# Projections with PSUM banks taken singly, the rotary embedding in two operations, and one operation less in the roots

## The chip, the cores and the metric

One core of a Trainium2 chip runs the whole kernel. The metric is the device time of one execution in microseconds. TensorE (PE) multiplies out of SBUF into PSUM, which has eight banks of 512 float32 columns; VectorE (DVE) and ScalarE (ACT) read PSUM; GpSimd (POOL) works in SBUF only here; SyncE (SP) issues nearly all of the transfers.

## The reference

Two encoder layers on 1024 tokens of width 1024. Each layer normalises its input and projects it with one matrix of 2848 columns, whose columns belong to three kinds of attention: latent attention (6 heads, with a second projection from a rank of 384 for the queries and 256 for keys and values), differential attention (4 heads with two maps each) and grouped-query attention with a rotary embedding in two axes (6 query heads, 2 key heads). Queries and keys are normalised per head and rotated:

```python
def _rms_norm(x, gain):
    y = xf * lax.rsqrt(jnp.mean(xf * xf, axis=-1, keepdims=True) + EPS)
    return (y * gain).astype(x.dtype)

def _apply_rope(x, cos, sin):
    half = x.shape[-1] // 2
    x1, x2 = xf[..., :half], xf[..., half:]
    return jnp.concatenate([x1 * cos - x2 * sin, x1 * sin + x2 * cos], axis=-1)

for l in range(DEPTH):
    h = _rms_norm(x, attn_norm[l]) @ w_in[l]
    (h_cq, h_ckv, h_kr, h_dq, h_dk, h_dv, h_gq, h_gk, h_gv) = jnp.split(h, IN_OFFSETS, axis=-1)
    ...
    x = x + mix @ w_o[l]
    gate, up = jnp.split(_rms_norm(x, ffn_norm[l]) @ w_gate_up[l], 2, axis=-1)
    x = x + (jax.nn.silu(gate) * up) @ w_down[l]
```

The attentions are dense softmax attentions without a mask, with scale width^-0.5.

## The kernel before, in words

Each float32 operand of a large product is split into a high part of TensorE's rounded float32 type and the rest, and `mm3` (line 162) issues three matmuls: rest by high, high by rest, high by high. They have the lines 164, 165 and 166 in the profile.

A layer has four stages in this order: the projections, the attention, the output projection, and the feed-forward part (whose products are arranged so that seven block products do the work of eight). The change lies in the projections, and in small operations elsewhere.

**Projections.** The tokens lie in 8 tiles of 128. `x_features` (244) transposes the input in 8 pieces for each half of the tokens: four 128 by 128 transposes into one PSUM bank (`pt`, line 248), then ACT writes the high part (250) and DVE the rest (251, tile `xl`). `weights` (225) loads two k-tiles of a weight slice at a time on SP's queue (232), ACT casts the high part (`wh`, through `split`, line 123) and POOL or DVE makes the rest (`wl`, line 124). `project` (302) then takes the token tiles in pairs: for both it issues all matmuls over k into the two halves of one PSUM tile of two banks (`psb`), and then calls `emit` for both. `emit` is the reader of the projection. In `heads64` (404) it is: ACT copies PSUM to `raw` with the row's scale (415), DVE rotates (349 and 351), POOL adds the two rotary products (418), ACT squares (419), DVE sums the squares per head (420), and, for the grouped-query slice that also carries values, ACT and DVE write the values' two parts from PSUM (437, 438). In `mla_q` (490) it is ACT's copy (499), POOL's gain (504), the rotary, POOL's sum (512), and the squares. `mla_kv` (523) reads keys by 537 and values by 123 and 124 (tile `vst`). `down` (453) reads by DVE (461), and the shared rotary key goes through `kr_extra` (553).

After each half of the tokens `finish` (383) takes the root of the mean squares and POOL multiplies it on (391). `out_features`, which transposes the result for the attention (368) and stores it in two parts (ACT 372, DVE 373, tiles `sth` and `stl`, transfers 381), is put off: `project` calls it once LAG steps of later products have been issued. `neg_lambda` (178) makes one small product per layer.

**The rotary** (`rope`, 344): `dst = raw * C` in one DVE operation, and `tmp` = the swapped halves by the signed sine in two operations, one for each half. `rotate64` (396) calls it for each group of 2 × `half` columns of a head of 64, so once for a differential head (half 32) and twice for a grouped-query head (half 16).

**The roots** (`newton`, 126): a first guess by integer operations (132, 133), h = -0.5 v (135), and three steps of r·r, times h, and (t + 1.5)·r (138, 139, 140), all dependent, on DVE. With `eng` given (the outputs of the differential heads) the steps run on POOL with four operations a step and no h. `rsq` (148) makes v = ssq / n + eps (151) and calls it; `finish` multiplies the attention's scale on in an operation of its own (389).

**PSUM.** One pool at a time holds the eight banks. `psum(2, 2)` for the projections: two tiles `s` of two banks for the products, two banks `t` for the transposes of `out_features`, two banks `o`; `x_features` takes `o` and `t` in turn, `neg_lambda` takes `o`. `psum(3, 1)` (637) for the attention. `psum_one()` (989) for the rest: three banks `u` and five banks `v`; its tiles are used singly. At the layer's end `psum(2, 2)` comes again (1325).

**What sets the order.** Each engine works through its instructions in a fixed order, laid out when the program is built: the framework places instructions by the program's order and by when their inputs and buffers come free on a simulated timeline. SP's transfers are in a fixed order too. Work buffers of the projections are two deep (`raw`, `tmp`, `vst`), the weights' parts six.

Of the kernel before, what the change touches and what calls it, by code (L numbers as in the profile page):

```python
# [12 lines left out]
F32 = mybir.dt.float32  # L13
# [3 lines left out]
ALU = mybir.AluOpType  # L17
# [3 lines left out]
P = 128  # L21
# [44 lines left out]
def encoder(ctx: ExitStack, tc: tile.TileContext, a: dict, out: bass.AP):  # L66
# [22 lines left out]
    def ps_o(name, n=512):  # L89
        return banks["pool"].tile([P, n], F32, tag="o", name=name, bufs=banks["o"])  # L90

    def psum_one():

        banks["pool"].release()
        banks["pool"] = tc.alloc_tile_pool(name="psu", bufs=3, space=PSUM, reuse_waits="tile")

    def ps_u(name):
# [28 lines left out]
    def newton(pool, v, n, tag, eng=None):  # L126

        i = pool.tile([P, n], I32, tag=tag + "i", name="i")
        h = pool.tile([P, n], F32, tag=tag + "h", name="h")
        t = pool.tile([P, n], F32, tag=tag + "t", name="t")  # L130
        r = pool.tile([P, n], F32, tag=tag + "r", name="r")
        ve.tensor_scalar(i, v.bitcast(I32), 1, None, ALU.arith_shift_right)
        ve.tensor_scalar(r.bitcast(I32), i, -1, 0x5F3759DF, ALU.mult, ALU.add)
        if eng is None:
            ve.tensor_scalar(h, v, -0.5, None, ALU.mult)
        for _ in range(3):
            if eng is None:
                ve.tensor_tensor(out=t, in0=r, in1=r, op=ALU.mult)
                ve.tensor_tensor(out=t, in0=t, in1=h, op=ALU.mult)
                ve.scalar_tensor_tensor(out=r, in0=t, scalar=1.5, in1=r, op0=ALU.add, op1=ALU.mult)  # L140
            else:
                eng.tensor_tensor(out=t, in0=r, in1=r, op=ALU.mult)
                eng.tensor_tensor(out=t, in0=t, in1=v, op=ALU.mult)
                eng.tensor_scalar(t, t, -0.5, 1.5, ALU.mult, ALU.add)
                eng.tensor_tensor(out=r, in0=t, in1=r, op=ALU.mult)
        return r

    def rsq(pool, ssq, n, inv, scale, tag):

        v = pool.tile([P, n], F32, tag=tag + "v", name="v")  # L150
        ve.tensor_scalar(v, ssq, inv, EPS, ALU.mult, ALU.add)
        r = newton(pool, v, n, tag)
        if scale != 1.0:
            ve.tensor_scalar(r, r, float(scale), None, ALU.mult)
        return r

    def gain_cols(src, n, name):
        t = lay.tile([P, n], F32, tag=name, name=name)
# [19 lines left out]
    def neg_lambda(l):  # L178
        lam_init = 0.8 - 0.6 * math.exp(-0.3 * l)
        lq = lay.tile([64, 4], F32, tag="lq", name="lq")  # L180
        for i, n in enumerate(("diff_lq1", "diff_lq2", "diff_lk1", "diff_lk2")):
            sy.dma_start(out=lq[:, i : i + 1], in_=a[n][l].unsqueeze(1))
        lp = lay.tile([64, 2], F32, tag="lp", name="lp")
        ve.tensor_mul(lp, lq[:, 0:2], lq[:, 2:4])
        pl_ = ps_o("pl_")
        pe.matmul(pl_[:, 0:2], ones[:64, :], lp, start=True, stop=True)
        le = lay.tile([P, 2], F32, tag="le", name="le")
        ac.activation(le, pl_[:, 0:2], AF.Exp)
        nlam = lay.tile([P, 1], F32, tag="nlam", name="nlam")
        ve.tensor_tensor(out=nlam, in0=le[:, 1:2], in1=le[:, 0:1], op=ALU.subtract)  # L190
        ve.tensor_scalar(nlam, nlam, -lam_init, None, ALU.add)
        return nlam

    psum(2, 2)
    def rows_by_quarters(t):

        return lambda tt, c0, c1: t[tt // 4][c0 // 512][:, tt % 4, c0 % 512 : (c1 - 1) % 512 + 1]
# [5 lines left out]
    for l in range(L):  # L203
# [39 lines left out]

        def x_features(g):
            for j in range(KT):
                pt = ps_t("pt") if j % 2 else ps_o("pt")
                for i in range(4):
                    pe.transpose(pt[:, i * P : (i + 1) * P], Xv(4 * g + i, j * P, (j + 1) * P), ident)
                h, lo = (t[:, j, :] for t in XT[g])
                ac.activation(h, pt, AF.Copy, scale=g_attn[:, j : j + 1])  # L250
                ve.scalar_tensor_tensor(
                    out=lo, in0=pt, scalar=g_attn[:, j : j + 1], in1=f(h), op0=ALU.mult, op1=ALU.subtract
                )
# [48 lines left out]
        def project(x, nk, w, n, emit):  # L302
            (xh, xl), (wh, wl) = x, w
            for tp in range(TT // 2):
                ps = ps_s("psb")
                for i in range(2):
                    for k in range(nk):
                        mm3(
                            ps[:, i, :n], xh(k, 2 * tp + i), xl(k, 2 * tp + i), wh[k], wl[k],
                            k == 0, k == nk - 1,  # L310
                        )
                for i in range(2):
                    emit(2 * tp + i, ps[:, i, :n])
                for e in list(later):
                    e[0] -= nk * n
                    if e[0] < 0:
                        later.remove(e)
                        e[1]()
                yield
# [24 lines left out]
        def rope(raw, half, C, Sn, dst, tmp):  # L344

            shape = list(raw.shape)
            C, Sn = (t.unsqueeze(1).to_broadcast(shape) for t in (C, Sn))
            cut = slice(0, half), slice(half, 2 * half)
            ve.tensor_tensor(out=dst, in0=raw, in1=C, op=ALU.mult)
            for c in range(2):  # L350
                ve.tensor_tensor(
                    out=tmp[:, :, cut[c]], in0=raw[:, :, cut[1 - c]], in1=Sn[:, :, cut[c]], op=ALU.mult
                )

        def work(name, n, most=384):
            return bp.tile([P, n], F32, tag=name, name=name, padded_shape=[P, most])
# [6 lines left out]

        def out_features(g, t, pieces, gains=None):
            for j, (c0, w, rows) in enumerate(pieces):
                pt = ps_t("pt")
                for i in range(4):
                    pe.transpose(pt[:w, i * P : (i + 1) * P], t[:, i, c0 : c0 + w], ident)
                h = bp.tile([P, 512], F32R, tag="sth", name="sth")[:w]
# [13 lines left out]
        def finish(g, t, ssq, nh, width, pieces, scaled):  # L383

            n = 4 * nh
            r = rsq(bp, ssq.rearrange("p t h -> p (t h)"), n, 1.0 / width, 1.0, "q")
            if scaled:
                rv = r.rearrange("p (t h) -> p t h", h=nh)[:, :, :scaled]
                ve.tensor_scalar(rv, rv, float(width**-0.5), None, ALU.mult)
            tv = t.rearrange("p t (h x) -> p (t h) x", x=width)  # L390
            po.tensor_tensor(
                out=tv, in0=tv, in1=r.unsqueeze(2).to_broadcast([P, n, width]), op=ALU.mult
            )
            later.append([LAG, lambda: out_features(g, t, pieces)])

        def rotate64(raw, t, tmp, h0, h1, C, Sn, half, tt):
            for b in range(0, 64, 2 * half):
                rv, tv, mv = (
                    x.rearrange("p (h x) -> p h x", x=64)[:, h0:h1, b : b + 2 * half]
                    for x in (raw, t, tmp)  # L400
                )
                rope(rv, half, C[:, tt, b : b + 2 * half], Sn[:, tt, b : b + 2 * half], tv, mv)

        def heads64(col, nh, extra, tables, half, pieces, scaled, emit_extra=None):

# [916 lines left out]
                        sy.dma_start(out=out[0, r0 : r0 + P, cs], in_=x)  # L1322
        op_.release()
        fp.release()
        psum(2, 2)
        if l < L - 1:
            xin = dram.tile([S, D], F32, tag="xs", name="xs", bufs=1)
            for r in range(2):
# [29 lines left out]
```

## Time and profile before

| | us |
|---|---|
| median of three runs | 3275.53 |
| lowest and highest | 3267.33, 3277.81 |
| the profiled execution | 3267.01 |
| its span, first to last instruction | 3265.2 |

The profile shows one execution. The busy line gives each engine's busy time, its share of the span and its instructions. A row of busy time by stretches gives the same for a part of the span, and the clock that TensorE was granted there as a share of full speed. In the waits and in brackets in the timeline stands how long an engine was idle before an instruction, and what ended that. In the timeline a row with x2 is two instructions of one kind in a row. The first layer's projections run from the start to about 400 us, the second layer's from about 1640 to 2022 us.

### The profile page before, as it was taken

Reading aid. Unit: us, or ns where it says so; the run is one execution under the profiler, and the core shown is the slowest. Engines: PE = TensorE matmul, PEld = TensorE weight load, DVE = VectorE, ACT = ScalarE, POOL = GpSimd, SP = SyncE. Lnnn points to the kernel's source line nnn. Section 1 sums busy time; section 2 is a strip of 40 time slices with the busy share of each in tenths; the row PEclk is TensorE's granted clock in tenths of the full one; section 3 lists DMA queues with packets and bytes.
Section 4 is the critical chain, followed back from the end, with each engine's and each line's share of the span. In section 5 each row is a group of like instructions: output and inputs, shape, how many; then the busy total and the mean of one; then the engine's idle time right before and its main releaser. Section 6 shows DMA issues by size and latency. Waiting matters only on the chain.

```text
span 3265.2 us, 50229 instructions
## 1 busy us (share of the span) xinstructions
PE 3096.9 (95%) x17628; PEld 2712.1 (83%) x17628; DVE 2319.8 (71%) x4560; ACT 1586.5 (49%) x3010; POOL 1139.7 (35%) x1562
## 2 busy tenths in 40 slices
PE   8889899999998999989998888999999989999999
PEld 7888888888787888878887888888887878888787
DVE  5976788888537656667669777888884476656776
ACT  4433378887424333333343344888773343333332
POOL 1633477777302001000026344777772021001000
PEclk9999999999999999999999999999999999999999
DMA  4565534333662333374344656434346523334632
GB/s 145 162 202 172 177 118 129 113 105 113 217 220 76 102 97 101 116 263 143 97 136 150 191 179 189 122 112 118 109 142 207 187 74 105 109 97 160 221 134 100
DMA packets 386076, 466.17 MB, mean 143 GB/s; under 512 B 36768, under 2 KB 275360, under 8 KB 385824
## 3 DMA queue, kind: packets, MB, share of 16 engines
q1 hardware_dynamic: 372416, 418.38, 41.3%
q0 software_dynamic: 13408, 44.57, 4.1%
q8 instruction: 140, 2.29, 0.3%
q14 instruction: 112, 0.92, 0.1%
HBM read 313.42 MB, written 149.42 MB: 142 GB/s over the span
## 4 chain that ended last, share of the span: by engine, by line
PE 76%; DVE 11%; DMA 5%; ACT 3%; issue 3%; POOL 1%; SPq 1%; ACTq 0%; DVEq 0%; POOLq 0%
PE sc L688 8%; PE pv L897 8%; PE ptc L711 5%; PE psa L164 5%; PE psa L166 5%; PE psa L165 5%; PE psb L164 4%; PE psb L165 4%; PE psb L166 4%; PE psy L166 4%; PE psy L165 4%; PE psy L164 4%; PE psc L166 2%; PE psc L164 2%; PE psc L165 2%
## 5 line engine op out<-in xcount | busy, mean ns | idle before, releaser
L688 PE MATMUL sc<-k,q 128*128 128x512 f32 (+1 forms) x1472 | 418.6, 413 | 14.7 <-ACT p L696 14.1
L695 DVE TENSOR_REDUCE nm<-sc 128x1 f32<-128x1024 f32 x320 | 389.7, 1218 | 56.9 <-PE sc L688 53.8
L164 PE MATMUL psb<-wh,xl 128*128 128x256 f32 (+2 forms) x1280 | 388.9, 305 | 40.2 <-DVE vst L438 12.8
L696 ACT ACTIVATE p<-sc,nm 128x1024 f32<-128x1024 f32 x320 | 359.0, 1122 | 61.6 <-DVE nm L695 48.7
L165 PE MATMUL psb<-wl,xh 128*128 128x256 f32 (+2 forms) x1280 | 386.2, 302 | 2.5 <-POOL wl L124 2.0
L166 PE MATMUL psb<-wh,xh 128*128 128x256 f32 (+2 forms) x1280 | 384.6, 300 | 0.0
L717 DVE TENSOR_TENSOR pl<-ptc,ph 128x512 fp32r<-128x512 f32 x512 | 336.7, 681 | 28.0 <-ACT ph L716 26.3
L716 ACT CAST ph<-ptc 128x512 fp32r<-128x512 f32 x512 | 287.4, 587 | 79.1 <-PE ptc L711 70.8
L688 PEld LDWEIGHTS sc<-k,q 128*128 128x128 f32 (+1 forms) x1472 | 257.9, 191 | 63.5 <-ACT p L696 24.2
L711 PE MATMUL ptc<-ident,p 128*128 128x128 f32 x2048 | 290.9, 275 | 12.0 <-DVE pl L717 6.5
L897 PE MATMUL pv<-ph,v 128*128 128x256 f32 x1280 | 299.4, 286 | 0.0
L164 PEld LDWEIGHTS psb<-wh,xl 128*128 128x128 f32 x1280 | 249.8, 196 | 44.5 <-issue 13.4
L897 PE MATMUL pv<-pl,v 128*128 128x256 f32 x1024 | 275.4, 294 | 8.4 <-DVE ot L763 6.4
L711 PEld LDWEIGHTS ptc<-ident,p 128*128 128x128 f32 x2048 | 241.0, 142 | 46.2 <-DVE pl L717 6.3
L1229 POOL DMA_DIRECT2D hd<-h x66 | 36.1, 547 | 680.0 <-DVE h L1170 434.3
L164 PE MATMUL psy<-bh,al 128*128 128x512 f32 x616 | 240.9, 394 | 14.9 <-DVE al L124 14.9
L165 PEld LDWEIGHTS psb<-wl,xh 128*128 128x128 f32 x1280 | 249.7, 195 | 3.8 <-POOL wl L124 2.8
L751 POOL TENSOR_SCALAR p<-p,rec 128x1024 f32<-128x1024 f32 x192 | 215.7, 1127 | 104.5 <-DVE rec L701 83.4
L166 PEld LDWEIGHTS psb<-wh,xh 128*128 128x128 f32 x1280 | 249.4, 195 | 0.0
L165 PE MATMUL psy<-bl,ah 128*128 128x512 f32 x616 | 241.2, 392 | 0.1
L166 PE MATMUL psy<-bh,ah 128*128 128x512 f32 x616 | 240.4, 391 | 0.0
L123 ACT CAST wh<-ws 128x512 fp32r<-128x512 f32 x176 | 108.6, 623 | 265.1 <-PE psa L166 236.4
(223 smaller groups left out, 7687.5 us busy)
## 6 DMA issues: line engine op xcount, KB each, us to landing
graw<-in_w_gate_up SPq DMA_DIRECT2D x88, 512.0 KB, 5.4
ar<-hd SPq DMA_DIRECT2D x28, 1024.0 KB, 6.1
hd<-hs POOLq DMA_DIRECT2D x88, 256.0 KB, 3.1
hd<-h POOLq DMA_DIRECT2D x66, 256.0 KB, 2.4
q<-qd SPq DMA_DIRECT2D x256, 64.0 KB, 2.4
B<-od SPq DMA_DIRECT2D x12, 1280.0 KB, 7.0
wraw<-in_w_in SPq DMA_DIRECT2D x56, 256.0 KB, 3.2
o<-od SPq DMA_DIRECT2D x10, 1280.0 KB, 11.0
```

Of the source, the lines that this page charges most:

```text
L123: (hi_eng or ac.copy)(h, src)
L164: pe.matmul(ps, xl, wh, start=first, stop=False, skip_group_check=more)
L165: pe.matmul(ps, xh, wl, start=False, stop=False, skip_group_check=more)
L166: pe.matmul(ps, xh, wh, start=False, stop=last, skip_group_check=more)
L688: pe.matmul(ps[:, half, :], q[x][:, cut], kk[y], start=at == 0, stop=at == len(products) - 1)
L695: ve.tensor_reduce(nm, pf, axis=AX.X, op=ALU.max, negate=True)
L696: ac.activation(p, pf, AF.Exp, bias=nm, accum_out=s)
L711: pe.transpose(pt[:, k * P : (k + 1) * P], p[:, (4 * b + k) * P : (4 * b + k + 1) * P], ident)
L716: ac.copy(h, pv)
L717: ve.tensor_tensor(out=pl[:, 4 * b : 4 * b + 4, i * P : (i + 1) * P], in0=pv, in1=f(h), op=ALU.subtract,)
L751: po.tensor_scalar(p, p, r, 1.0, ALU.mult, ALU.mult)
L897: pe.matmul(b.o, x, y, start=first, stop=last)
```

## The change

Four edits:

- PSUM: `project` takes one bank `v` for each token tile (five deep) in place of a half of a tile of two banks (two deep). All transposes of the projections and the product of `neg_lambda` take banks `u` (three deep). The pool `psum_one` now serves the projections, too, and stays from the output projection of one layer to the projections of the next.
- Rotary: the two operations for the halves become one, which reads the halves in reversed order; `rotate64` calls `rope` once for 64 columns, so that the product with C is one operation for the whole head, and for a half of 16 two reversed ones follow.
- Roots on DVE: -0.5 goes into the first operation of a step, and h is gone.
- Scale: `rsq` folds a scale into v, so that `finish` needs operation 389 only where it applies to some of the heads.

```diff
     def psum_one():
-        banks["pool"].release()
+        if banks:
+            banks["pool"].release()
...
     def newton(pool, v, n, tag, eng=None):
-        h = pool.tile([P, n], F32, tag=tag + "h", name="h")
...
-        if eng is None:
-            ve.tensor_scalar(h, v, -0.5, None, ALU.mult)
         for _ in range(3):
             if eng is None:
-                ve.tensor_tensor(out=t, in0=r, in1=r, op=ALU.mult)
-                ve.tensor_tensor(out=t, in0=t, in1=h, op=ALU.mult)
+                ve.scalar_tensor_tensor(out=t, in0=r, scalar=-0.5, in1=r, op0=ALU.mult, op1=ALU.mult)
+                ve.tensor_tensor(out=t, in0=t, in1=v, op=ALU.mult)
                 ve.scalar_tensor_tensor(out=r, in0=t, scalar=1.5, in1=r, op0=ALU.add, op1=ALU.mult)
...
     def rsq(pool, ssq, n, inv, scale, tag):
-        ve.tensor_scalar(v, ssq, inv, EPS, ALU.mult, ALU.add)
-        r = newton(pool, v, n, tag)
-        if scale != 1.0:
-            ve.tensor_scalar(r, r, float(scale), None, ALU.mult)
-        return r
+        ve.tensor_scalar(v, ssq, inv / scale**2, EPS / scale**2, ALU.mult, ALU.add)
+        return newton(pool, v, n, tag)
...
-        pl_ = ps_o("pl_")
+        pl_ = ps_u("pl_")
...
-    psum(2, 2)
+    psum_one()
...
-                pt = ps_t("pt") if j % 2 else ps_o("pt")
+                pt = ps_u("pt")
...
-                ps = ps_s("psb")
+                ps = [ps_v("psb")[:, :n] for _ in range(2)]
                 for i in range(2):
                     for k in range(nk):
                         mm3(
-                            ps[:, i, :n], xh(k, 2 * tp + i), xl(k, 2 * tp + i), wh[k], wl[k],
+                            ps[i], xh(k, 2 * tp + i), xl(k, 2 * tp + i), wh[k], wl[k],
                             k == 0, k == nk - 1,
                         )
                 for i in range(2):
-                    emit(2 * tp + i, ps[:, i, :n])
+                    emit(2 * tp + i, ps[i])
...
         def rope(raw, half, C, Sn, dst, tmp):
             shape = list(raw.shape)
-            C, Sn = (t.unsqueeze(1).to_broadcast(shape) for t in (C, Sn))
-            cut = slice(0, half), slice(half, 2 * half)
-            ve.tensor_tensor(out=dst, in0=raw, in1=C, op=ALU.mult)
-            for c in range(2):
-                ve.tensor_tensor(
-                    out=tmp[:, :, cut[c]], in0=raw[:, :, cut[1 - c]], in1=Sn[:, :, cut[c]], op=ALU.mult
-                )
+            n = shape[2]
+            ve.tensor_tensor(out=dst, in0=raw, in1=C.unsqueeze(1).to_broadcast(shape), op=ALU.mult)
+            for b in range(0, n, 2 * half):
+                cut = (slice(None), slice(None), slice(b, b + 2 * half))
+                rv, tv = (t[cut].rearrange("p h (c x) -> p h c x", c=2) for t in (raw, tmp))
+                sv = Sn[:, b : b + 2 * half].rearrange("p (c x) -> p c x", c=2).unsqueeze(1)
+                ve.tensor_tensor(out=tv, in0=rv[:, :, ::-1, :], in1=sv.to_broadcast(list(rv.shape)), op=ALU.mult)
...
         def out_features(g, t, pieces, gains=None):
-                pt = ps_t("pt")
+                pt = ps_u("pt")
...
         def finish(g, t, ssq, nh, width, pieces, scaled):
-            r = rsq(bp, ssq.rearrange("p t h -> p (t h)"), n, 1.0 / width, 1.0, "q")
-            if scaled:
+            whole = width**-0.5 if scaled == nh else 1.0
+            r = rsq(bp, ssq.rearrange("p t h -> p (t h)"), n, 1.0 / width, whole, "q")
+            if 0 < scaled < nh:
...
         def rotate64(raw, t, tmp, h0, h1, C, Sn, half, tt):
-            for b in range(0, 64, 2 * half):
-                rv, tv, mv = (
-                    x.rearrange("p (h x) -> p h x", x=64)[:, h0:h1, b : b + 2 * half]
-                    for x in (raw, t, tmp)
-                )
-                rope(rv, half, C[:, tt, b : b + 2 * half], Sn[:, tt, b : b + 2 * half], tv, mv)
+            rv, tv, mv = (x.rearrange("p (h x) -> p h x", x=64)[:, h0:h1, :] for x in (raw, t, tmp))
+            rope(rv, half, C[:, tt, :], Sn[:, tt, :], tv, mv)
...
         op_.release()
         fp.release()
-        psum(2, 2)
         if l < L - 1:
```

## The prediction

> **What bounds the kernel now.** I read the page's busy line first, then busy time by stretches, then who waited for whom, then single stalls in the timeline.
>
> ```profile
> PE 3096.9 (95%) x17628; PEld 2712.1 (83%) x17628; DVE 2319.8 (71%) x4560; ACT 1586.5 (49%) x3010; POOL 1139.7 (35%) x1562
> ```
>
> TensorE is the bound, so a change can only win where it stands idle or at a lower clock. The stretches (columns: start and end, length, busy time of PE, PEld, DVE, ACT, POOL with counts, granted clock, DMA share, GB/s) show where that is:
>
> ```profile
> 30.00:400.00 370.00, 333.09 (x2385) 326.81 (x2385) 276.05 (x931) 140.56 (x359) 163.94 (x166) 0.95 0.53 166
> 1662.00:2020.00 358.00, 320.40 (x2349) 313.99 (x2349) 271.98 (x923) 140.39 (x359) 162.46 (x165) 0.96 0.55 169
> 2020.00:3265.00 1245.00, 1205.58 (x6365) 1022.13 (x6363) 872.45 (x1314) 631.30 (x1097) 400.88 (x607) 0.99 0.43 134
> ```
>
> The first two rows are the projections of the two layers, which is all that the change touches. PE is idle there for 36.9 and 37.6 us, and the clock of 0.95 and 0.96 loses 18.5 and 14.3 us more. So 107 us is the most that can be had. VectorE is busy for 75% of it and cannot be the bound on average; it must be late at moments. The waits over the whole span (us in total, times, longest) name them:
>
> ```profile
> PE pt L368 <- DVE stl L373: 16.2, 7, 5.9
> ...
> PE psb L164 <- DVE vst L438: 12.8, 2, 6.5
> PE psb L164 <- ACT vst L437: 12.6, 2, 6.4
> PE psb L164 <- ACT raw L499: 11.9, 7, 3.9
> PE pt L248 <- DVE xl L251: 8.1, 6, 2.7
> PE psb L164 <- DVE vst L124: 7.7, 4, 2.5
> ```
>
> Four of the six rows are matmuls of a projection (psb) waiting for a reader of a PSUM tile: 45.0 us. The rest are transposes waiting for their bank.
>
> **Banks singly.** Before, a projection tile is two banks for two token tiles, two such tiles deep. The reader of the first half waits for both halves:
>
> ```profile
> 346.18 0.28 PE L166 MATMUL psb<-wh,xh 128*128 128x256 f32 x1
> ...
> 346.56 0.84 ACT L415 ACTIVATE raw<-psb,r 128x256 f32<-128x256 f32 x2 [8.46 <-PE psb L166]
> ```
>
> Both copies (x2) start behind the pair's last matmul, and both banks are given back only after the second token tile is read. After, there are five single banks, each given back by itself. The prices of a bank come from stretches that hold nothing but such matmuls, the clock from the stretches behind a stall:
>
> ```profile
> 241.30:248.00 6.70, 6.66 (x23) 6.69 (x24) 6.49 (x39) 2.27 (x6) 1.59 (x3) 0.57 0.65 229
> 248.00:258.00 10.00, 10.00 (x60) 9.97 (x59) 5.78 (x38) 2.31 (x7) 3.35 (x3) 1.00 0.05 16
> 376.20:386.20 10.00, 10.00 (x86) 10.00 (x85) 8.87 (x37) 1.71 (x4) 4.47 (x4) 1.00 0.47 165
> 147.20:150.00 2.80, 0.00 (x0) 0.00 (x0) 2.80 (x9) 0.64 (x2) 1.60 (x3) 1.00 0.48 183
> 151.50:154.90 3.40, 3.40 (x17) 3.40 (x16) 3.40 (x15) 2.20 (x5) 2.96 (x4) 0.50 0.19 59
> 154.90:164.50 9.60, 9.60 (x75) 9.60 (x75) 9.10 (x35) 1.48 (x4) 6.72 (x10) 1.00 0.28 83
> ```
>
> Sixty matmuls of 384 columns take 10.0 us, so a bank (8 k by 3 products, 24 matmuls) is 4.0 us; 86 of 256 columns take 10.0 us, a bank 2.8 us; 75 of 288 columns take 9.6 us, a bank of the first up-projection (9 matmuls) 1.15 us.
>
> The stall that ends at 241.34:
>
> ```profile
> 232.89 0.84 ACT L123 CAST wh<-wraw 128x768 fp32r<-128x768 f32 x1 [12.35 <-DMA wraw<-in_mla_w_ukv]
> 233.91 0.62 ACT L123 CAST wh<-wraw 128x512 fp32r<-128x512 f32 x1 [0.17 <-DMA wraw<-in_w_in]
> 234.44 0.47 ACT L415 ACTIVATE raw<-psb,r 128x256 f32<-128x256 f32 x1
> ...
> 238.28 0.34 DVE L438 SCALAR_TENSOR_TENSOR vst<-psb,r,vst 128x128 fp32r<-128x128 f32 x1
> ...
> 241.34 0.66 PE L164 MATMUL psb<-wh,xl 128*128 128x384 f32 x1 [6.21 <-ACT vst L437]
> ```
>
> ScalarE held the readers back for 12.35 us behind a weight cast, and PE stopped at 235.1 with both pairs full. With a fifth bank it works on to 235.1 + 4.0 = 239.1, and the first token tile's bank is free at 238.28 + 0.34 = 238.6. The whole 6.2 us goes, and with it the clock behind: 0.43 of 6.7 us, 2.9 us. That is 9.1 us a layer.
>
> The stall that ends at 270.17:
>
> ```profile
> 263.99 0.34 DVE L438 SCALAR_TENSOR_TENSOR vst<-psb,r,vst 128x128 fp32r<-128x128 f32 x1
> ...
> 269.69 0.34 DVE L438 SCALAR_TENSOR_TENSOR vst<-psb,r,vst 128x128 fp32r<-128x128 f32 x1
> ...
> 270.17 0.55 PE L164 MATMUL psb<-wh,xl 128*128 128x256 f32 x1 [6.34 <-DVE vst L438]
> ```
>
> PE waited for the second token tile (read at 270.0), though the first had been read at 264.3. The fifth bank gives 2.8 us of work, the first tile's bank another 2.8. What comes next, the banks of the second up-projection, queues behind the same readers, so some is given back: bounds 2.8 and 5.6, I take the middle, 4.2 us a layer. Both layers show the pair of stalls (two times each in the waits): 2 × (9.1 + 4.2) = 26.6 us.
>
> The seven waits for raw L499 (11.9 us) are the first up-projection, where ACT, DVE and POOL per token tile are slower than PE's 1.15 us. One bank more takes at most 1.15 us from each, 8.0 in all; some are shorter than that, I take 6. The 2.8 us without PE (147.2 to 150.0) is followed by 3.4 us at clock 0.50, which costs 1.7 us; with two such waits halved, 1.7 us returns. [...]
>
> The four waits for vst L124 are at most 2.5 us long, under one bank of 2.8 us: 7.7 us goes.
>
> **Transposes.** They move from 2 banks (4 in the input's own transposes, which take turns in two sets) to 3 shared ones. Of the 16.2 us of waits on stl L373, a third bank lets one piece more start, but the data it transposes and the next piece hang on the same VectorE queue: bounds 0 and 16.2, I take 2 us, near nothing, because of that queue. The input's transposes lose a bank: they wait six times today, 1.35 us on average; bounds 0 and the same 8.1 us once more, I take 4 us lost. The small product for lambda moves from the one set into the other; it is one tile a layer, taken at nothing.
>
> **Rotary and roots.** VectorE's stream around a rotary:
>
> ```profile
> 140.62 0.41 DVE L349 TENSOR_TENSOR half<-raw,tab 128x256 f32<-128x256 f32 x1
> 140.95 0.48 DVE L351 TENSOR_TENSOR tmp<-raw,tab 128x128 f32<-128x128 f32 x2
> 141.35 0.42 DVE L349 TENSOR_TENSOR half<-raw,tab 128x256 f32<-128x256 f32 x1
> ```
>
> Starts lie 0.33 us apart for 256 elements and 0.40 us for twice 128, so joining two operations saves 0.07 us. Per layer: 32 token tiles of differential heads save 1 operation each, 8 of gqa_q 3, 8 of gqa_rest 6, 16 of mla_q 1, 8 of the shared key 1: 128 operations, 9.0 us. The trace has no operand read backwards; the halves are already read swapped at no extra cost, so I take a reversed order at the same price, with up to twice the time as the other end. The 26 roots a layer each lose one small operation off the dependent chain, 0.07 us by the same saving, 1.8 us; ten lose the scaling at the chain's end (0.17 us, next fence), 1.7 us. Together 12.5 us of VectorE a layer. None stands on PE's path by itself, as VectorE is idle for a quarter of the stretch; it counts inside the waits already priced, and I add nothing.
>
> **Sum.** 26.6 + 6 + 1.7 + 7.7 + 2 - 4 = 40.0 us. The profiled execution took 3267.0 us (span 3265.2), 8.5 us under the median of 3275.5; it would take 3227, and the median 3235.5.
>
> **The rivals.** (1) VectorE's backlog, not the banks, is the limit, and the fifth bank only moves each stall by 3 us.
>
> ```profile
> 122.02 0.17 DVE L389 TENSOR_SCALAR r<-r 128x12 f32<-128x12 f32 x1
> 122.10 2.67 DVE L349 TENSOR_TENSOR half<-raw,tab 128x256 f32<-128x256 f32 x2
> 122.34 2.15 POOL L391 TENSOR_TENSOR half<-half,r 128x1152 f32<-128x1152 f32 x1 [4.07 <-DVE r L389]
> ```
>
> Two operations that need 0.75 us took 2.67 while POOL ran for 2.15. POOL is busy for 164 of 370 us, and in that share it is POOL's time, not the number of operations, that VectorE pays. The rotary's 9.0 us would shrink to 9.0 × 206 / 370 = 5.0, with the roots 8.5 us a layer, half of it where PE waits: 8.5 us in all, 3267 us. For it: all of PE's idle 2.8 us above had VectorE busy throughout. Against: the two long stalls had a bank free early. [...]
>
> (2) The queues of ACT and DVE keep their order by pairs, so that the release by single banks is lost and only the fifth bank counts: 2 × (4.0 + 2.8) + 6 + 7.7 - 4 = 23.3 us, 3252 us. For it: the program still issues both readers behind both products.
>
> (3) Everything on those rows goes: 12.8 + 12.6 + 11.9 + 7.7 + 16.2 = 61.2 us, and the clock in proportion, 32.8 × 61.2 / 74.5 = 27 us: 3187 us. It needs the transposes' waits to go too, which hang on VectorE.
>
> (4) Slower: the order of ACT's queue is laid out anew, and the weight casts come ahead of the readers oftener.
>
> ```profile
> ACT wh L123 <- DMA wraw<-in_w_in: 15.2, 11, 3.3
> ACT wh L123 <- DMA wraw<-in_mla_w_ukv: 14.3, 2, 12.4
> ```
>
> These are 29.5 us of ScalarE's idle time in the first layer's stretch, in which it reads no bank. If half of it becomes new idle time of PE, that is 29.5 us over two layers, while the 26.6 us of the two stalls stay: 29.5 - 13.4 = 16 us slower, 3292 us. It decides once more than 13 us of these waits reach PE beyond today's. Against: five banks hold 14 to 20 us of work.
>
> **How the numbers follow.** My case has a chance of 0.56 (own range 3210 to 3255), the rivals 0.16, 0.12, 0.08 and 0.08. What a measurement of this kernel can tell from no change is about 0.3%, 10 us. Faster: my case, (2) and (3) whole, and 0.07 of (1), 0.83. The same: 0.09 of (1), 0.01 of (4), 0.10. Slower: 0.07. The range of 3197 to 3268 leaves out most of (3), all of (4) and a little of (1), under 2 in 10.
>
> **What would show it.** Right: the rows psb on vst L438 and L437 nearly vanish, the projections' clock rises to 0.97 or more, and readers follow their own bank instead of the pair. Rotary operations of 256 elements stay near 0.42 us in the clear. Wrong: the idle time of PE in the projections stays near 37 us a layer under other names (weights, transposes), or the joined operations take 0.6 us and more.

## The result and the profile after

The changed kernel takes 3217.36 us (median of 4 runs, 3214.76 to 3220.11) against 3274.78 us for the kernel before beside it: a ratio of 0.9833, 95% interval 0.9819 to 0.9847. The profiled execution took 3216.48 us (span 3214.7), 50.5 us less than the profiled one of before.

The busy line of the page after:

```profile
PE 3080.5 (96%) x17628; PEld 2697.1 (84%) x17628; DVE 2317.8 (72%) x4224; ACT 1586.4 (49%) x3010; POOL 1137.4 (35%) x1562
```

VectorE has 336 instructions fewer, but its busy time hardly fell (2319.8 before). That is the first sign that its time is not the sum of its instructions.

The stretches below run from a layer's first transposes to its first scores, so that each pair holds the same matmuls (columns as before). The first layer before and after, then the second:

```profile
5.00:399.80 394.80, 348.24 (x2458) 339.04 (x2459) 288.52 (x968) 160.72 (x407) 167.59 (x168) 0.94 0.54 171
5.00:373.40 368.40, 339.22 (x2458) 329.74 (x2458) 288.28 (x804) 162.88 (x409) 167.98 (x168) 0.98 0.60 185
...
1641.00:2020.70 379.70, 338.65 (x2462) 329.76 (x2460) 288.71 (x965) 157.58 (x396) 168.16 (x169) 0.96 0.55 169
1612.50:1969.30 356.80, 331.33 (x2463) 323.77 (x2461) 288.96 (x801) 160.28 (x401) 168.62 (x169) 0.99 0.59 182
```

The projections became 26.4 and 22.9 us shorter. PE's idle time there fell from 46.6 and 41.1 to 29.2 and 25.5 us. Its busy time for the same matmuls fell by 9.0 and 7.3 us, while the clock rose from 0.94 and 0.96 to 0.98 and 0.99. From a layer's first scores on, little changed: 1241.2 to 1239.1 us in the first layer, 1244.5 to 1245.4 in the second.

PE's waits after, over the whole span:

```profile
PE pt L364 <- DVE stl L369: 17.7, 9, 5.8
...
PE psb L160 <- POOL wl L125: 7.5, 8, 1.8
PE pt L364 <- POOL half L388: 7.2, 7, 1.7
PE pt L244 <- DVE xl L247: 6.9, 7, 1.9
...
PE psb L159 <- ACT wh L124: 4.8, 7, 1.9
...
PE sc L681 <- ACT le L183: 3.4, 1, 3.4
PE sc L681 <- DVE vst L431: 2.9, 1, 2.9
...
PE psb L159 <- DVE vst L125: 1.5, 3, 0.6
...
PE psb L159 <- ACT raw L492: 0.4, 2, 0.2
```

The two rows psb on vst that stood at 25.4 us before (L438 and L437, now L431 and L430) are gone; one wait of 2.9 us for the same reader now stands ahead of a layer's first scores (sc). raw went from 11.9 to 0.4. What is left in the projections are mostly transposes and weights. Three rows of before that the prediction did not show are needed to compare:

```profile
PE psb L164 <- ACT wh L123: 6.3, 3, 2.2
...
PE pt L368 <- POOL half L391: 2.8, 4, 1.1
PE psb L165 <- POOL wl L124: 2.0, 2, 1.3
```

### The profile page after: what moved, and what is told of

The parts are those of the page before. It is cut to its first block, busy times and chain, and to the rows that moved or that the text cites. A ratio compares the mean times of both kernels' runs of the same rounds, so it can differ in the third digit from the quotient of the medians.

```text
span 3214.7 us, 49930 instructions
## 1 busy us (share of the span) xinstructions
PE 3080.5 (96%) x17628; PEld 2697.1 (84%) x17628; DVE 2317.8 (72%) x4224; ACT 1586.4 (49%) x3010; POOL 1137.4 (35%) x1562
## 4 chain that ended last, share of the span: by engine, by line
PE 74%; DVE 12%; DMA 5%; ACT 3%; issue 3%; POOL 1%; SPq 1%; ACTq 0%; DVEq 0%; POOLq 0%
PE sc L681 8%; PE pv L890 8%; PE ptc L704 5%; PE psa L159 5%; PE psa L161 5%; PE psa L160 5%; PE psy L160 4%; PE psy L161 4%; PE psy L159 4%; PE psb L161 3%; PE psb L159 3%; PE psb L160 3%; PE psc L161 2%; PE psc L160 2%; PE psc L159 2%
## 5 line engine op out<-in xcount | busy, mean ns | idle before, releaser
L159 PE MATMUL psb<-wh,xl 128*128 128x256 f32 (+2 forms) x1280 | 381.1, 302 | 6.7 <-ACT wh L124 4.8
L160 PE MATMUL psb<-wl,xh 128*128 128x256 f32 (+2 forms) x1280 | 379.4, 298 | 7.7 <-POOL wl L125 7.5
L161 PE MATMUL psb<-wh,xh 128*128 128x256 f32 (+2 forms) x1280 | 377.4, 297 | 0.0
L124 ACT CAST wh<-ws 128x512 fp32r<-128x512 f32 x176 | 108.5, 622 | 266.9 <-PE psa L161 236.0
## 6 DMA issues: line engine op xcount, KB each, us to landing
o<-od SPq DMA_DIRECT2D x10, 1280.0 KB, 11.5
```

The lines of the kernel that those rows point to most:

```text
L124: (hi_eng or ac.copy)(h, src)
L159: pe.matmul(ps, xl, wh, start=first, stop=False, skip_group_check=more)
L160: pe.matmul(ps, xh, wl, start=False, stop=False, skip_group_check=more)
L161: pe.matmul(ps, xh, wh, start=False, stop=last, skip_group_check=more)
```

## The experiments

Times are medians; the time of the kernel before on the same chip was 3271.0 us for the first four, 3269.7 for the next four, 3272.0 for the last four.

| kernel | us | ratio to before (95%) |
|---|---|---|
| the change | 3217.4 | 0.9833 (0.9819 to 0.9847) |
| 1 banks only | 3233.7 | 0.9883 (0.9868 to 0.9898) |
| 2 rotary and roots, old banks | 3232.7 | 0.9876 (0.9859 to 0.9892) |
| 3 the change with four single banks | 3212.6 | 0.9816 (0.9801 to 0.9831) |
| 4 the change with pairs | 3241.1 | 0.9906 (0.9891 to 0.9920) |
| 5 rotary only | 3243.5 | 0.9917 (0.9903 to 0.9930) |
| 6 roots only | 3265.6 | 0.9990 (0.9981 to 0.9999) |
| 7 four single banks, four for transposes | 3206.9 | 0.9806 (0.9792 to 0.9819) |
| 8 the change, squares summed on ScalarE | 3211.3 | 0.9821 (0.9807 to 0.9834) |
| 9 as 7, lambda early | 3205.7 | 0.9800 (0.9782 to 0.9817) |
| 10 as 9, squares on ScalarE | 3201.2 | 0.9786 (0.9768 to 0.9804) |
| 11 the change without GpSimd's scaling | 3175.0 | 0.9709 (0.9689 to 0.9730) |
| 12 as 10, transposes later | 3210.7 | 0.9817 (0.9800 to 0.9834) |

**1 and 2: the two halves of the change.** Kernel 1 has all hunks on PSUM and the old rotary and roots; kernel 2 has the new rotary and roots and the old PSUM.

```diff
 kernel 1, against before:
-                ps = ps_s("psb")
+                ps = [ps_v("psb")[:, :n] for _ in range(2)]
...
-                pt = ps_t("pt")
+                pt = ps_u("pt")
```

> The kernel before with the PSUM part of the change alone: banks singly (five for the products, three shared by the transposes), rotary in three operations and roots as before. Theory A (the banks are the whole gain; the 336 operations fewer on VectorE lie beside TensorE's work): 3210 to 3225 us, the rows psb on vst L438 and L437 gone. Rival B (VectorE's backlog: the shorter rotary and roots give a part of the 57 us): 3230 us or more, with the missing part back on waits of transposes for stl.

> Rotary in two operations and the shorter roots, with the PSUM pairs of the kernel before. Theory A: within 8 us of before (3267 to 3283 us), the two long stalls per layer (psb on vst, 25.4 us together) still there. Rival B: 3255 us or less.

Measured: 1.17% and 1.24% faster, together 1.67%. Theory A fell: rotary and roots alone gain as much as the banks alone. Nor do the two add up: 2.41% less 1.67% is 0.74%, 24 us, that both remove. In part they are two remedies for the same stalls: the rows psb on vst, 25.4 us before, are gone in kernel 1 and at 18.3 in kernel 2. The first layer's stretch (before and after in the section on the result), with the banks only,

```profile
5.00:378.80 373.80, 339.45 (x2459) 328.73 (x2459) 300.59 (x968) 163.81 (x409) 167.16 (x168) 0.98 0.58 183
```

and with rotary and roots only:

```profile
5.00:383.90 378.90, 344.85 (x2457) 336.83 (x2458) 275.94 (x804) 159.74 (x407) 169.40 (x168) 0.95 0.57 177
```

The busy time of VectorE stands third behind the length. The new rotary and roots take 12.6 us off it (288.5 to 275.9). The banks put 12.1 us on it, with the same 968 instructions. So with both it is where it was. (The expectations below speak of 27 us a layer: those are sums over groups, which count operations that overlap twice; the windows count time once.)

What the change gains beyond kernel 1 lies for the largest part (15.2 to 7.2 us) in the transposes that wait for GpSimd's scaling of a half:

```profile
PE pt L370 <- POOL half L393: 15.2, 14, 2.6
```

**3 and 4: what about the banks counts.** Both keep the new rotary, the new roots and three shared transpose banks, and leave one bank unused. The lines give the edits in effect.

```diff
 kernel 3, against the change (in the projections):
-        ... tag="v", name=name, bufs=5)
+        ... tag="v", name=name, bufs=4)
 kernel 4, against the change:
-                ps = [ps_v("psb")[:, :n] for _ in range(2)]
+                ps = ps_s("psb")    # two pairs
```

> The changed kernel with four single banks for the projections instead of five and one bank unused; three shared transpose banks. It parts the release of single banks from the fifth bank. Theory A1 (both count, as in my working: of the stall of 6.2 us at 241.34 the release at 238.6 takes 2.7, the bank of 4.0 us the rest): about half of the gain stays, 3235 to 3250 us. Rival C (the queues keep the order of pairs, only the fifth bank counts): 3262 us or more. Rival D (only the release counts, the fifth bank is never the one that is missing): within 5 us of 3217.

> The changed kernel's rotary, roots and three shared transpose banks, but the projections in two pairs of banks as before (one bank unused). Theory A: like the kernel with the old banks altogether, 3265 to 3280 us, as a third bank for transposes was priced at 2 us gained and one bank less for the input's transposes at 4 us lost. Rival E (the third transpose bank is a large part of the gain): 3255 us or less, with the row pt on stl (16.2 us before) halved.

Four banks in two pairs: 3241.1 us. The same four singly: 3212.6. Single banks are worth 28.5 us beside the new rotary, and the fifth bank nothing that shows (0.9816 with four, 0.9833 with five, intervals that overlap). Rival D's number was right, rival C fell. PE's waits in kernel 4, with pairs,

```profile
PE psb L159 <- DVE vst L431: 17.4, 5, 4.6
```

and in kernel 3, with four single banks:

```profile
PE psb L160 <- ACT raw L493: 6.4, 6, 1.6
...
PE psb L160 <- DVE vst L432: 0.5, 1, 0.5
PE psb L161 <- POOL wl L126: 0.4, 2, 0.3
```

The stalls on vst go with the single banks. For raw, however, the fifth bank is missed (7.2 us in kernel 4, 6.4 with four single banks, 0.4 with five); what it takes there comes back in other rows, such as the weights on GpSimd (0.4 with four, 7.5 with five).

The stretch of the two long stalls, from the first matmul of the grouped-query key and value projection on, with the same products in both but for a few transposes, in kernel 4 and in kernel 3:

```profile
210.16:286.63 76.47, 67.41 (x420) 66.14 (x419) 51.10 (x173) 25.66 (x66) 32.15 (x30) 0.93 0.62 189
```

```profile
204.13:271.29 67.16, 64.06 (x413) 62.94 (x412) 52.35 (x169) 23.81 (x63) 31.53 (x29) 0.97 0.70 215
```

PE is idle for 3.1 us in place of 9.1. The release is not all that differs, though: with other banks the program was laid out anew. In kernel 4, as before, ScalarE's cast of a weight stands ahead of this projection's first reader:

```profile
225.33 0.83 ACT L124 CAST wh<-wraw 128x768 fp32r<-128x768 f32 x1 [11.72 <-DMA wraw<-in_mla_w_ukv]
...
227.29 0.47 ACT L408 ACTIVATE raw<-psb,r 128x256 f32<-128x256 f32 x1
```

In kernel 3 one reader stands ahead of the cast, and the cast waits for less:

```profile
211.00 0.47 ACT L409 ACTIVATE raw<-psb,r 128x256 f32<-128x256 f32 x1 [5.65 <-PE psb L162]
...
219.20 0.84 ACT L125 CAST wh<-wraw 128x768 fp32r<-128x768 f32 x1 [7.16 <-DMA wraw<-in_mla_w_ukv]
```

How much of the 28.5 us is the release and how much this order, no run parts. In kernel 1 the cast is still ahead of all these readers and waits for 11.2 us, and the stalls on vst are gone even so, but there with five banks.

Kernel 4 is 8.4 us slower than kernel 2, which has the same pairs and 2 + 2 banks for transposes. The intervals just overlap (0.9859 to 0.9892 and 0.9891 to 0.9920). Neither theory had that, and its cause stays open; the extra transpose bank was no gain there.

**5 and 6: rotary or roots.**

```diff
 kernel 5, against before: only rope and rotate64
+                ve.tensor_tensor(out=tv, in0=rv[:, :, ::-1, :], in1=sv..., op=ALU.mult)
 kernel 6, against before: only newton, rsq and finish
```

> The kernel before with the rotary in two operations alone (old banks, old roots). The runs so far: the banks alone give 37 us, rotary and roots alone 38 us, all together 57 us, so the theory that VectorE's saving adds nothing has fallen. Theory F: PE waits for readers that stand in VectorE's queue; every us that this queue gets shorter counts, wherever it stands in it. The rotary has about two thirds of VectorE's saving (18 of some 27 us a layer by the groups of the profiles), so 24 to 30 us of the 38: 3241 to 3247 us. Rival G: the chain of the root, on which the half tile's scaling and then the transposes hang, is what counts; then the rotary gives under 12 us: 3259 us or more.

> The kernel before with the shorter roots alone. Theory F: about a third of the 38 us, 3257 to 3264 us. Rival G (the root's chain counts): 3247 us or less.

Rotary: 26.2 us. Roots: 4.1 us, at the edge of what can be told. Theory F's number holds for the rotary and was too high for the roots, and its reason ("wherever it stands") falls with them: VectorE's busy time in the whole kernel fell by 6.0 us in kernel 5 and by 5.6 in kernel 6 (2319.8 to 2313.8 and 2314.2). So it is not the amount. The place can be seen in part. The stretch of the two long stalls before and in kernel 5:

```profile
215.88:297.86 81.98, 68.26 (x420) 66.72 (x419) 56.57 (x232) 25.76 (x66) 32.88 (x30) 0.92 0.59 181
```

```profile
210.10:288.09 77.99, 67.60 (x420) 65.78 (x419) 54.58 (x177) 25.39 (x66) 33.27 (x30) 0.93 0.63 189
```

In the second layer it is 81.6 and 74.2 us. So 11.4 of the 28.0 us by which kernel 5's projections are shorter lie here, and the rest is spread over them. In kernel 6 this stretch takes 83.2 and 81.5 us: the roots gain nothing in it.

Around the first long stall, VectorE before:

```profile
234.94 0.79 DVE L349 TENSOR_TENSOR half<-raw,tab 128x64 f32<-128x64 f32 x1 [2.11 <-ACT raw L415]
...
238.28 0.34 DVE L438 SCALAR_TENSOR_TENSOR vst<-psb,r,vst 128x128 fp32r<-128x128 f32 x1
239.16 0.23 DVE L349 TENSOR_TENSOR half<-raw,tab 128x64 f32<-128x64 f32 x1 [0.54 <-ACT raw L415]
...
240.85 0.35 DVE L438 SCALAR_TENSOR_TENSOR vst<-psb,r,vst 128x128 fp32r<-128x128 f32 x1
```

and in kernel 5:

```profile
227.28 1.54 DVE L348 TENSOR_TENSOR half<-raw,tab 128x128 f32<-128x128 f32 x1 [0.66 <-ACT raw L411]
...
230.55 0.34 DVE L434 SCALAR_TENSOR_TENSOR vst<-psb,r,vst 128x128 fp32r<-128x128 f32 x1
...
231.43 0.29 DVE L348 TENSOR_TENSOR half<-raw,tab 128x128 f32<-128x128 f32 x1 [0.21 <-ACT raw L411]
...
232.39 0.34 DVE L434 SCALAR_TENSOR_TENSOR vst<-psb,r,vst 128x128 fp32r<-128x128 f32 x1
```

Before, twelve rotary operations of a token tile and a sum stand ahead of the reader vst; in kernel 5 six rotary operations do. For the second tile that is 1.7 and 1.0 us (239.16 to 240.85, 231.43 to 232.39), but for the first it is 3.3 us in both, for in kernel 5 some of its operations are long (1.54 us on 128 elements at 227.28, where the next of its kind took 0.28). PE's stall shrank from 6.2 to 3.1 us. From ScalarE's first copy to the end of the second reader it is 6.8 us before and 6.0 in kernel 5, so the operations ahead of the reader explain 0.8 us. The other 2.3 lie ahead of the copy, which starts 0.7 us ahead of PE's stop before and 3.0 us in kernel 5. It stands behind the weight cast, whose wait for its transfer fell from 12.4 us (in the prediction) to 9.0, of which a second cast gave some back (0.2 to 2.0):

```profile
ACT wh L123 <- DMA wraw<-in_mla_w_ukv: 11.6, 2, 9.0
```

Why this weight came earlier, no run shows. That fewer operations stand ahead of a reader is thus a small part of what the rotary is worth, and where most of its 26 us come from stays open.

**7: a fourth transpose bank in place of the fifth for the products.** In effect:

```diff
-        ... tag="v", name=name, bufs=5)
+        ... tag="v", name=name, bufs=4)
-        ... tag="u", name=name)            # 3
+        ... tag="u", name=name, bufs=4)
```

> The changed kernel with four single banks for the projections and four for the transposes (the bank that lay idle in the kernel with four single banks). Theory F and the loss of 8 us that the pairs showed from a fourth to a third transpose bank: 3202 to 3210 us, the row pt on stl (15.5 us with three) at 10 us or less. Rival (the pieces wait for VectorE's queue whatever the banks, as my prediction had it): 3211 to 3215 us, like the one with four and three.

The time, 3206.9 us, lies in the first range, but the row pt on stl stayed at 12.1 us (six times) against the 10 expected, and the gain over four and three is within the intervals. Against the change (0.9833) the intervals just touch.

**8: sums of squares to ScalarE.**

```diff
-                ac.activation(sq, raw, AF.Square)
-                ve.tensor_reduce(ssq, sq.rearrange(...), axis=AX.X, op=ALU.add)
+                for h in range(nh):
+                    hs = slice(64 * h, 64 * h + 64)
+                    ac.activation(sq[:, hs], raw[:, hs], AF.Square, accum_out=ssq[:, h : h + 1])
```

> The changed kernel with the sums of squares per head taken by ScalarE while it squares (one activation per head) instead of a reduction on VectorE: 80 operations, 31.6 us a layer by the groups L413, L509 and L537, leave VectorE; ScalarE, at 143 of 336 us, gets 80 operations of one head instead of a whole token tile's. Theory F: with single banks 27 us a layer less on VectorE were worth 16 us (3234 to 3217), so about 19 us here: 3195 to 3205 us. Rival H (ScalarE's queue is as late as VectorE's at the moments that count, and the three more small operations per token tile hold its casts and copies back): 3215 us or more, with waits of psb on ACT up.

Six us less than the change, intervals overlapping. The time lies between the two forecasts, so neither theory F nor rival H had it. VectorE's busy time in the first layer fell from 288.3 to 268.6, ScalarE's rose from 162.9 to 206.7 us. A square over the whole token tile in the change:

```profile
L412 ACT ACTIVATE sq<-raw 128x256 f32<-128x256 f32 x48 | 20.0, 419 | 3.8 <-DVE ssq L413 1.9 <-DVE r L138 0.9 <-DVE v L149 0.4
```

became four over one head each, and each of them is followed by a second instruction of 0.19 us, by its name the read of the sum:

```profile
L414 ACT ACTIVATE sq<-raw 128x64 f32<-128x64 f32 x192 | 46.7, 247 | 0.7
L414 ACT ACTIVATION_READ_ACCUMULATOR sq<-raw 128x1 f32 x192 | 36.6, 191 | 0.0
```

**9, 10 and 12: on from there.** Kernel 9 issues the product for lambda ahead of the last transposes; 10 adds the squares of kernel 8; 12 holds the transposes of a finished half back for longer.

```diff
 kernel 9, against kernel 7:
+        lq = lambda_rows(l)        # the four loads
         run(diff_v(1))
+        nlam = neg_lambda(l, lq)
         for _, e in later:
             e()
-        nlam = neg_lambda(l)
 kernel 12, against kernel 10:
-        LAG = 6000
+        LAG = 8000
```

> Four single banks for projections and four for transposes, and the small product for lambda moved ahead of the last transposes of the stage (its four small loads ahead of the last value projection). In that kernel without the move PE waited 6.2 us in two places for ACT le L184, where the first scores of a layer take over the bank of the lambda product. Theory L (I had taken this at nothing; the product now queues behind the transposes' readers): these waits go, 3206.9 becomes 3200 to 3203 us. Rival: the first scores wait for the last transposes' readers instead (stl, or the values' vst), and the time stays at 3205 to 3209 us.

> The same with the sums of squares on ScalarE, which took 27 us a layer off VectorE in the changed kernel and 6 us off the time there. Theory F: 4 to 8 us less than the kernel with four and four banks and lambda early, 3193 to 3199 us. Rival: with four transpose banks VectorE's queue no longer shows at PE, no difference within 3 us.

> The kernel with four and four banks, lambda early and squares on ScalarE, with the transposes of a finished half held back for 8000 instead of 6000 columns of products. Theory: the row pt on stl, the largest wait of the projections, is partly transposes issued before their data are scaled, so that later ones wait less: 3 to 8 us faster than that kernel. Rival: the readers of the transposes queue on VectorE wherever they are put, within 3 us; or the held tiles (three) run out and the time goes up.

Kernel 9: no difference (the rival's range), and the scores still waited for the lambda product's reader, 6.7 us in two places (6.2 in kernel 7). So moving the product ahead of these transposes does not take that wait away. Kernel 10: 3201.2 us, 4.5 us under kernel 9 and within its interval, but below the change beyond both intervals. It is the fastest complete version here: 2.14% under before, where the change is 1.67%. Its transposes hardly wait for stl any more (2.4 us).

Kernel 12 was 9.5 us slower than 10, each of its runs slower than each of kernel 10's. Its transposes wait as little, but another wait grew from 1.1 us: the up-projection reads back the features that these transposes write.

```profile
PE psb L160 <- DMA lat<-cqd: 13.7, 2, 7.9
```

**11: what GpSimd's work costs VectorE.** This kernel leaves out the multiplication of each finished half by its root, so q and k go out unscaled.

```diff
-            po.tensor_tensor(
-                out=tv, in0=tv, in1=r.unsqueeze(2).to_broadcast([P, n, width]), op=ALU.mult
-            )
```

> The changed kernel without GpSimd's multiplication of each finished half tile by its root (left out, so q and k go out unscaled): 20 operations of 2.06 us, 41 us of GpSimd a layer. VectorE's own operations are the same. Theory P (VectorE's operations with two operands in SBUF stretch while GpSimd runs): VectorE's busy time in the projections falls by 10 us a layer or more from 335, and the rotary's 256-element operations (mean 0.70 and 0.81 us, at least 0.41) come down; the time by 8 to 20 us, partly because transposes hang on this scaling. Rival (the long durations are not GpSimd's doing): VectorE's busy time stays within 3 us.

```profile
5.00:351.70 346.70, 331.88 (x2459) 324.96 (x2459) 262.35 (x804) 163.87 (x409) 127.90 (x148) 1.00 0.63 197
```

GpSimd has 40 us less to do in this layer; VectorE, with the same 804 instructions, is busy for 26 us less (288.3 to 262.4). The stretch is 22 us shorter, and the kernel over both layers 42 us. The rotary's products with the sine, of 256 elements, in the change,

```profile
L349 DVE TENSOR_TENSOR tmp<-raw,tab 128x256 f32<-128x256 f32 x32 | 25.8, 806 | 0.0
```

and without the scaling:

```profile
L349 DVE TENSOR_TENSOR tmp<-raw,tab 128x256 f32<-128x256 f32 x32 | 17.6, 551 | 0.0
```

The products with the cosine fell less (mean 700 to 669 ns). The means hide two kinds. In the change 22 of these 32 operations took 0.41 or 0.42 us and ten took 0.82 to 2.34; without the scaling, five did. Each of the ten started 0.11 to 0.25 us after an operation of GpSimd's and ended 0.28 us after its end, as here:

```profile
80.83 1.95 POOL L388 TENSOR_TENSOR half<-half,r 128x1024 f32<-128x1024 f32 x1 [1.02 <-DVE r L138]
80.94 2.13 DVE L349 TENSOR_TENSOR tmp<-raw,tab 128x256 f32<-128x256 f32 x1
```

So these operations look held until GpSimd's end, and not slowed down all along. Where VectorE's started first it took 0.41 or 0.42 us; three that started second did so, too, and why is open.

Theory P's numbers hold, with more than it asked for. That two operands in SBUF are needed for it, no run shows: in the change operations with one tensor input lasted until GpSimd's end, too (last section). How much of the 42 us is VectorE's and how much the transposes that no longer wait for the scaling, this run does not part. By these numbers each us of this GpSimd work went with some 0.65 us of VectorE's busy time (26 / 40).

The same is the likely reason why kernel 1 costs VectorE 12 us for nothing: its operations are the ones of before, but took longer each. Before, and in kernel 1:

```profile
L351 DVE TENSOR_TENSOR tmp<-raw,tab 128x128 f32<-128x128 f32 x64 | 29.2, 498 | 0.2 <-ACT raw L415 0.2
```

```profile
L353 DVE TENSOR_TENSOR tmp<-raw,tab 128x128 f32<-128x128 f32 x64 | 32.1, 540 | 0.0
```

GpSimd is as busy in both (167.6 and 167.2 us), in 21 us less. The traces of this stretch show more time in which both are busy at once, 148.5 us in place of 131.6, though an operation that waits also adds to that. No run parts the two.

## Why the prediction was right, and where it was not

The forecast of 3235.5 us was 18 us high; the time lies in the range. The sum was 40.0 us between profiled executions; it is 50.5.

**The two long stalls (26.6 us).** The rows went, 25.4 us of waits and the clock behind them, and 2.9 us came back ahead of the first scores. But the step "With a fifth bank it works on to 235.1 + 4.0 = 239.1" named the wrong half of the remedy: four single banks do it as well as five, two pairs do not (experiments 3 and 4). The first tile of the pair was read at 238.6, in the second stall at 264.3, and PE went on at 241.34 and 270.17; with pairs these waits for vst are 17.4 us (kernel 4), with the same four banks singly 0.5 (kernel 3). The sum also took the order on ScalarE as it was; with single banks and the new rotary a reader moved ahead of the weight cast, and the runs do not part that from the release.

**raw L499 (6 us and 1.7 of clock).** 11.5 us went (11.9 to 0.4). I had given each wait one bank more, and here the fifth bank counts: pairs leave 7.2 us (kernel 4), four single banks 6.4 (kernel 3), five 0.4. So the step held, with 5.5 us more than forecast, of which the shorter rotary and roots may be a part: with old ones five banks leave 3.8 (kernel 1).

**vst L124 (7.7 us).** 6.2 went.

**Transposes (+2, -4).** The waits on stl rose from 16.2 to 17.7 us, 1.5 us outside the lower bound of the gain, 0. The longest one after the change shows the queue on VectorE that the prediction named as the reason:

```profile
153.44 2.12 POOL L388 TENSOR_TENSOR half<-half,r 128x1152 f32<-128x1152 f32 x1 [1.49 <-DVE r L138]
...
153.86 1.72 DVE L149 TENSOR_SCALAR v<-ssq 128x12 f32<-128x12 f32 x1
155.51 1.29 POOL L125 TENSOR_TENSOR wl<-wraw,wh 128x512 fp32r<-128x512 f32 x1
155.62 1.21 DVE L132 TENSOR_SCALAR i<-v 128x12 int32<-128x12 int32 x1
...
156.94 0.17 DVE L133 TENSOR_SCALAR r<-i 128x12 int32<-128x12 int32 x1
...
160.37 0.69 DVE L336 TENSOR_TENSOR tab<-tab,gsw 128x512 f32<-128x512 f32 x1 [0.73 <-DMA tab<-in_tables]
...
162.06 1.27 DVE L369 TENSOR_TENSOR stl<-pt,sth 128x512 fp32r<-128x512 f32 x2
...
162.88 1.06 PE L364 MATMUL pt<-ident,half 128*96 128x128 f32 x4 [5.76 <-DVE stl L369]
```

Ahead of the reader stl stand a root, tables and other halves. The input's transposes did not lose 4 us with one bank less; their row went from 8.1 to 6.9 us. With four (experiment 7) it is 3.6 us, and the time is within the intervals.

**What the sum did not have.** Weights on GpSimd (2.0 to 7.5), the half's scaling on GpSimd (2.8 to 7.2) and the lambda product, "taken at nothing" (0 to 3.4), cost 13.3 us more. They are next in line where the banks no longer hold PE up. wh gave 1.5 us back. So these rows: 25.4 + 11.5 + 6.2 - 1.5 + 1.2 - 13.3 + 1.5 = 31.0 us, where I had 32.5 without the clock. All of PE's idle time fell by 34.1 us (168.3 to 134.2, span less busy time); the rest are smaller rows.

**The clock was a mis-sized term.** I had 5.8 + 1.7 = 7.5 us of it. PE's busy time for the same 17628 matmuls fell from 3096.9 to 3080.5, by 16.4 us, which together with the 34.1 us of idle time is the whole 50.5. Of these, 16.3 us lie in the projections, where the granted clock rose (0.94 and 0.96 to 0.98 and 0.99). I had counted the clock only behind the waits whose slow stretch I had looked at.

**Rotary and roots: "None stands on PE's path by itself [...] I add nothing."** This step failed: beside the banks they add 16 us (3233.7 to 3217.4), nearly what the forecast lacked, and alone they gain 38, the rotary 26 of them. A mean idle share of a quarter said nothing about the moments when VectorE is late. Their saving on VectorE came out as worked out in kernel 2 (12.5 us a layer, 12.6 measured), but in the first layer it was 2.1 and 3.3 us in kernels 5 and 6 and 0.2 in the change, so that the agreement proves little.

The sum of 40.0 us was thus one for the banks, and the banks alone gave 37.4 (kernel 1). Even there two errors cancel in part, which is luck: between the profiled executions PE's idle time fell by 20.0 us, where I had 32.5, and its busy time by 12.7, where I had 7.5.

**The rivals.** (1), 3267 us, fell: the stalls did not merely move. With 40 us less of GpSimd's work VectorE was busy for 26 us less in the first layer (experiment 11), but the 8.5 us that (1) left for the rotary and the roots were too few: the rotary alone took 26 us off the kernel. (2), 3252 us, fell by experiments 3 and 4. (3), 3187 us, needed the transposes' waits to go; they stayed. (4), the casts ahead of the readers, did not come: wh on PE fell from 6.3 to 4.8 us, and the order that was laid out anew put a reader ahead of a cast. With the reversed operand an operation took what I had taken, 0.41 us in the clear. Yet the joined operations took 0.81 us in the mean, above the 0.6 that I had named as a sign of being wrong; that comes from the ten that stand beside GpSimd's operations, not from the order: the other 22 took 0.41 or 0.42 (experiment 11).

## What to carry to other kernels

Before adding buffers, look at how they are given back: the same four banks, taken singly instead of in pairs, were worth 28 us together with the order that was laid out for them, and a fifth nothing. A saving on an engine that is idle a quarter of the time was here neither nothing nor its size in busy time: rotary and roots, each alone, took 6.0 and 5.6 us off VectorE's busy time and were worth 26 and 4 us. When two parts of a change may cure the same stalls, time each alone: here 37 and 38 us made 57.

## What the hardware showed that I had not expected

- Some VectorE operations that met one of GpSimd's lasted until that one ended, even on 12 elements. In the last fence of the timeline, v<-ssq on 12 elements took 1.72 us and ended at 155.58, GpSimd's scaling at 155.56; the next, on 12 elements, took 1.21 us and ended at 156.83, GpSimd's 155.51 at 156.80. The one after them took 0.17 us. Both have one tensor input. Under experiment 11 stand ten more of the change's, of 0.82 to 2.34 us, and three that started beside a running operation of GpSimd's and took 0.41 us. Why VectorE's operation has to wait, these runs do not show.
- In kernel 8 each square that also sums is followed by an instruction of 0.19 us that reads the sum, nearly as long as the squares of 64 elements themselves (0.25 us). Four small ones with it in place of one (0.42 us) are 1.75 us.
